# Modulation sums on four column strips of TensorE, and another order of the last expert pair's work

## The chip, the cores and the metric
The kernel runs on one core of a Trainium2 chip. The metric is device time in microseconds of one launch. The core's engines appear in the rows as PE (TensorE, the matrix engine) with PEld (its weight loads), DVE (VectorE), ACT (ScalarE), POOL (GpSimd) and SP (SyncE, which here only issues DMAs). Each engine takes its instructions in order, and they wait for each other by semaphores.

## The reference, cut to what matters
A trunk of two layers over 256 tokens of width 1024. Both layers get their shifts, scales and gates from one conditioning vector:

```python
cond = jax.nn.silu(c)
for i in range(DEPTH):                                  # 2 layers
    mod = (cond @ ada_w[i] + ada_b[i])[:, None, :]      # 1024 -> 6 * 1024
    sh1, sc1, g1, sh2, sc2, g2 = jnp.split(mod, 6, axis=-1)
    x = x + g1 * mixer(rms_norm(x, gain[i, 0]) * (1 + sc1) + sh1)      # layer 0 GLA, layer 1 FoX
    x = x + g2 * ffn(rms_norm(x, gain[i, 1]) * (1 + sc2) + sh2)        # layer 0 dense, layer 1 MoE
# MoE: y = sum over 8 experts of combine_e * ((silu(h Wg_e) * (h Wu_e)) Wd_e), two experts for each token
```

A dense or expert SwiGLU is 1024 to 3584 and back. All weights are float32.

## The kernel before, in words
Weights come in tiles `raw` of 1 MB (128 partitions x 2048 numbers) by one DMA each, issued on SP's queue at L203 in program order, through a ring of 7 buffers, 10 in the expert stage. For most products a tile is split into two rounded parts, `whi` (ACT, L224) and `wlo` (DVE, L226), and every product is three matmuls: high by high, high by low, low by high (L241 to L243 with the activations held in the array, L247 to L249 with the weights held). A planner orders the instructions of each engine: it simulates the program and picks, among what is ready, what comes first in the program; functions marked `urgent` go ahead of that.

The modulations. One modulation (i, j) is 1024 numbers. `ada_gen` makes ten of them during the GLA and dense stages, a step at a time between the weight tiles: DVE multiplies each row block of `ada_w` by the conditioning value of its partition and adds it up in `adacc` (128x1024, L320 and L322). What is left is a sum over the 128 partitions and a turn from a row into columns, since `mod` is kept as 128 partitions x 8. `end` does both: for nine of the ten, eight matmuls that hold a 128-column block of `adacc` in the array and move one column of ones (L309), and `ada_out` adds the bias (L261). A float32 matmul stands in the trace as two records, so eight matmuls are 16. The tenth modulation, g2, takes another way (L304). The call of `end` for a modulation comes two steps into the next one.

The experts. They go in four pairs, ranked by their number of tokens on the device. Of a pair, `Large` x has up to 128 tokens and goes by the split parts; `Small` y has up to 64 tokens, takes `raw` as it is in float32, and `mm_s` (L1256) computes the two halves of the output columns in two strips of 64 array columns. The 3584 columns go in four chunks c (1024, 1024, 1024, 512): `gu` computes gate and up, `finish` turns the product (`actT`) for the down product, and `down` adds chunk c to the expert's output `md`. For chunk 3, `gu` has four weight tiles for the two halves together (two gate, two up) and `down` has two. Behind the last `down` of an expert, `scatter_pre` and `scatter` (x), or `scatter_s` (y), scale the output, split it, send it back to the tokens by one-hot matmuls (`sc`) and add it to `xres` (L1232 for x, L1210 for y). What is to be done later lies in a list, `pend`; `flush` runs it. The order of a pair is x.gu(0), y.gu(0), then for c = 0 to 2: x.down(c), x.gu(c+1), y.down(c), y.gu(c+1); then x.down(3). y.down(3) comes after the next pair's first x.gu(0), or, in the last pair, right behind x.down(3). Then `store` writes the output.

Of the kernel before, what the change touches and what calls it, by code (L numbers as in the profile page):

```python
# [17 lines left out]
P = 128  # L18
T = 256
NB = 2  # L20
D = 1024
KD = 8
FF = 3584
NFC = 7
NCH = 4
E = 8
# [24 lines left out]
def trunk(ctx, tc, x, c, ada_w, ada_b, norm_gain, gla_w_in, gla_w_gate_up, gla_b_gate, gla_o_norm, gla_w_out,  # L51
          fox_w_in, fox_b_f, fox_q_norm, fox_k_norm, fox_w_out, ffn_w_gate, ffn_w_up, ffn_w_down,
          moe_w_router, moe_b_router, moe_w_gate, moe_w_up, moe_w_down, out):
    nc = tc.nc
# [31 lines left out]
    def wk_ps(name):  # L86
        return pwk["p"].tile([P, 512], F32, tag="wkp", name=name)
# [4 lines left out]
    def bcast(ap, n):  # L92
        return bass.AP(tensor=ap.tensor, offset=ap.offset, ap=[[0, P], [1, n]])
# [9 lines left out]
    ident = cst.tile([P, P], F32, name="ident")  # L103
    make_identity(nc, ident)
    ones = cst.tile([P, P], F32, name="ones")
# [13 lines left out]
    bias = adap.tile([P, 96], F32, name="bias")  # L119
# [74 lines left out]
    def unit(src, nk):  # L194

        p = rawp
        if more["p"]:
            p = rawp if more["n"] % NRING < 7 else more["p"]
            more["n"] += 1
        raw = p.tile([P, 2048], F32, tag="raw", name="raw")  # L200
        v = raw.rearrange("p (k f) -> p k f", k=nk)
        for s, dst in src:
            ld.dma_start(dst(v), s.rearrange("(k p) f -> p k f", p=P))  # L203
        return v
# [52 lines left out]
    def ada_out(i, j, ps):  # L257

        c = (6 * i + j) * KD
        m = mod[i, j] = cst.tile([P, KD], F32, name=f"mod_{i}_{j}")  # L260
        nc.vector.tensor_add(m, ps, bias[:, c:c + KD])  # L261
        if j in (1, 4):
            g = (2 * i + j // 3) * KD
            nc.vector.tensor_mul(m, m, gain[:, g:g + KD])
# [33 lines left out]
    def ada_gen(todo):  # L298
        def end(i, j, a):
            if (i, j) == (1, 5):  # L300
                ld.dma_start(g2, bcast(ada_b[1:2, 5 * D:6 * D], D))
                for h in range(2):
                    ps = wk_ps(f"g2_{h}")
                    nc.tensor.matmul(ps, ones, a[:, h * 512:(h + 1) * 512], start=True, stop=True)  # L304
                    nc.vector.tensor_add(g2[:, h * 512:(h + 1) * 512], g2[:, h * 512:(h + 1) * 512], ps)
                return
            ps = wk_ps(f"adat_{i}_{j}")
            for k in range(KD):
                nc.tensor.matmul(ps[:, k:k + 1], a[:, k * P:(k + 1) * P], ones[:, 0:1], start=True, stop=True)  # L309
            ada_out(i, j, ps[:, 0:KD])  # L310

        late = None
        for i, j in todo:
            a = ada["p"].tile([P, D], F32, tag="adacc", name=f"adacc_{i}_{j}", bufs=2)
            for u in range(4):
                raw = unit([(ada_w[i][u * 2 * P:(u + 1) * 2 * P, j * D:(j + 1) * D], lambda v: v)], 2)
                for kk in range(2):
                    k = 2 * u + kk
                    if k == 0:
                        nc.vector.tensor_scalar(a, raw[:, kk, :], csil[:, k:k + 1], None, op0=ALU.mult)  # L320
                    else:
                        nc.vector.scalar_tensor_tensor(a, raw[:, kk, :], csil[:, k:k + 1], a, op0=ALU.mult, op1=ALU.add)  # L322
                if u == 1 and late:
                    end(*late)
                    late = None
                yield
            late = (i, j, a)
        end(*late)


# [768 lines left out]
    def experts(norm, wr):  # L1099
        rest, hh, hl, pos, comb, cmi, weights, ranks, first, order, pos_s, comb_s, room = route(norm, wr)  # L1100
        a, s = norm.a(), norm.s()
# [86 lines left out]
        def flush():  # L1188
            todo, pend[:] = pend[:], []
            for f in todo:  # L1190
                f()
# [189 lines left out]
        for e in range(0, E, 2):  # L1381
            x = Large(e)
            x.gu(0)
            tail()
            if e == 0:
                gather(1, 1)
            y = Small(e + 1)
            y.gu(0)
            for c in range(NCH - 1):
                x.down(c)  # L1390
                x.gu(c + 1)
                if (e, c) == (0, 0):
                    weights()
                y.down(c)
                y.gu(c + 1)
            if e + 2 < E:
                gather(e + 2, e + 3)
            x.down(NCH - 1, flush if e + 2 == E else lambda: None)

            def tail(y=y):  # L1400
                y.down(NCH - 1, flush)
# [77 lines left out]
    with wk.phase("first"):  # L1479
# [30 lines left out]
        h, step = n0.apply("X")  # L1510
# [25 lines left out]
    with wk.phase("fox"):  # L1536
        n3 = Norm("moe", "X", lambda: mod[1, 4], lambda: mod[1, 3])
        wr = side_by_side(small["wr_raw"], E, "wr")
        with wk.phase("fox_groups"):
            go, last = fox(n2, small["wf_raw"], lambda: None)  # L1540
            out_proj(go, fox_w_out[0], lambda: mod[1, 2], "foxo", n3, last, 2, (1,))
        with tc.tile_pool(name="rawq", bufs=NRING - 7) as more["p"], wk.phase("experts"):
            xres, hh, hl, pos, comb, cmi, room = experts(n3, wr)
# [31 lines left out]
```

## Time and profile before
| | us |
|---|---|
| median of 3 runs (1474.64 to 1475.36) | 1474.78 |
| the profiled execution, its own time | 1478.52 |
| its span in the trace | 1476.8 |
| PE busy | 1419.3 |
| DVE busy | 961.7 |
| ACT busy | 695.1 |

The trace is one execution, taken by the hardware profiler. Times in rows are us from the start of the span. A timeline row gives start, length, engine, line, operation, out<-in, held*moved or shapes, the count merged into the row, and in brackets how long the engine stood idle before and what ended that. The clock is the one granted to TensorE as a share of 2.4 GHz, so 0.50 is 1.2 GHz.

### The profile page before, as it was taken

The numbers are of one execution on the slowest core, as the hardware profiler recorded it, in microseconds if no ns is written. First come the engines' busy times: TensorE is split into PE (matmuls) and PEld (weight loads), VectorE is DVE, ScalarE is ACT, GpSimd is POOL, SyncE is SP. The second block draws the span as 40 slices with busy tenths as digits, with TensorE's granted clock in tenths as the row PEclk, the third lists the DMA queues.
The fourth block names the chain that finished last, engine by engine and source line by source line (L and its number), as shares of the span: only waits on it lengthen the run. The fifth ranks groups of instructions, "written<-read, shape, count | busy, mean of one in ns | idle before, by whom it ended". The sixth has DMA issues, their size and how long they took to land.

```text
span 1476.8 us, 21633 instructions
## 1 busy us (share of the span) xinstructions
PE 1419.3 (96%) x8443; PEld 1073.4 (73%) x8443; DVE 961.7 (65%) x1292; ACT 695.1 (47%) x982; POOL 80.5 (5%) x87
## 2 busy tenths in 40 slices
PE   6999999999999998999999999999999999999996
PEld 2899999999999997864756664656475556475453
DVE  7786897778977786662744764556574456574353
ACT  3653644344565565552644463445264346254241
POOL 2000200000132124000000000000000000000000
PEclk9999999999999999899999999999999999999998
DMA  9996578898865432699999999999999999999994
GB/s 318 362 340 226 189 269 313 296 345 279 286 178 161 127 103 86 252 403 395 409 402 402 409 409 409 409 402 402 409 409 409 409 401 404 409 409 408 410 398 189
DMA packets 183000, 488.86 MB, mean 331 GB/s; under 512 B 10815, under 2 KB 51913, under 8 KB 182890
## 3 DMA queue, kind: packets, MB, share of 16 engines
q1 hardware_dynamic: 182602, 486.87, 87.7%
q8 instruction: 68, 1.11, 0.3%
q10 hardware_dynamic: 288, 0.52, 0.1%
q14 instruction: 42, 0.34, 0.1%
HBM read 486.32 MB, written 1.05 MB: 330 GB/s over the span
## 4 chain that ended last, share of the span: by engine, by line
PE 81%; DMA 9%; DVE 7%; issue 1%; SPq 1%; ACT 0%; DVEq 0%; ACTq 0%
PE mo L1256 8%; PE mo L243 6%; PE mo L241 6%; PE mo L242 6%; PE md L1256 6%; DMA raw<-in_moe_w_up_dram 4%; PE gu L247 3%; DVE wlo L226 3%; PE gu L249 3%; PE gu L248 3%; PE md L243 3%; DMA raw<-in_moe_w_down_dram 3%; PE md L242 3%; PE md L241 3%; PE dn L247 2%; PE dn L248 2%
## 5 line engine op out<-in xcount | busy, mean ns | idle before, releaser
L226 DVE TENSOR_TENSOR wlo<-raw,whi 128x1024 fp32r<-128x1024 f32 (+2 forms) x481 | 569.0, 1232 | 92.2 <-ACT whi L224 90.9
L224 ACT CAST whi<-raw 128x1024 fp32r<-128x1024 f32 (+2 forms) x491 | 487.5, 1051 | 262.4 <-PE gu L248 67.3
L1256 PE MATMUL mo<-raw,gs 128*64 128x512 f32 (+1 forms) x1024 | 203.7, 543 | 9.9 <-DMA raw<-in_moe_w_up_dram 8.4
L241 PE MATMUL mo<-whi,g 128*128 128x512 f32 x448 | 175.9, 393 | 0.0
L242 PE MATMUL mo<-whi,g 128*128 128x512 f32 x448 | 175.5, 392 | 0.0
L1256 PEld LDWEIGHTS mo<-raw,gs 128*64 128x64 f32 x1024 | 70.3, 137 | 131.1 <-issue 95.5
L243 PE MATMUL mo<-wlo,g 128*128 128x512 f32 x448 | 153.0, 399 | 1.0 <-DVE wlo L226 0.5
L1352 DVE TENSOR_TENSOR msg<-msg,mo 128x512 f32<-128x512 f32 (+1 forms) x16 | 9.9, 620 | 171.6 <-PE mo L1256 171.6
L243 PEld LDWEIGHTS mo<-wlo,g 128*128 128x128 f32 x448 | 83.2, 189 | 35.9 <-issue 13.8
L1256 PE MATMUL md<-raw,gs 128*64 128x512 f32 x448 | 108.8, 603 | 0.0
L241 PEld LDWEIGHTS mo<-whi,g 128*128 128x128 f32 x448 | 84.6, 189 | 19.2 <-issue 1.6
L242 PEld LDWEIGHTS mo<-whi,g 128*128 128x128 f32 x448 | 84.7, 189 | 18.1
L322 DVE SCALAR_TENSOR_TENSOR adacc<-raw,csil,adacc 128x1024 f32<-128x1024 f32 x70 | 90.0, 1286 | 10.3 <-DMA raw<-in_ada_w_dram 9.9
L249 PE MATMUL gu<-h_ffn_h,wlo 128*128 128x256 f32 x320 | 90.5, 284 | 0.0
L248 PE MATMUL gu<-h_ffn_l,whi 128*128 128x256 f32 x320 | 90.1, 282 | 0.0
L247 PE MATMUL gu<-h_ffn_h,whi 128*128 128x256 f32 x320 | 89.9, 283 | 0.0
L241 PE MATMUL md<-whi,act_h 128*128 128x512 f32 x192 | 76.7, 400 | 0.5 <-ACT whi L224 0.5
L242 PE MATMUL md<-whi,act_l 128*128 128x512 f32 x192 | 76.1, 397 | 0.0
L1350 ACT ACTIVATE msg<-mo 128x512 f32<-128x512 f32 (+1 forms) x16 | 8.7, 544 | 132.6 <-PE mo L1256 132.6
L1175 ACT CAST act_h<-actT 128x512 fp32r<-128x512 f32 x24 | 13.3, 589 | 116.2 <-PE actT L1240 116.2
L1256 PEld LDWEIGHTS md<-raw,gs 128*64 128x64 f32 x448 | 28.2, 136 | 51.5 <-issue 51.2
L243 PE MATMUL md<-wlo,act_h 128*128 128x512 f32 x192 | 62.2, 398 | 1.4 <-DVE wlo L226 1.3
(488 smaller groups left out, 2706.1 us busy)
## 6 DMA issues: line engine op xcount, KB each, us to landing
raw<-in_moe_w_gate_dram SPq DMA_DIRECT2D x112, 1024.0 KB, 17.1
raw<-in_moe_w_up_dram SPq DMA_DIRECT2D x112, 1024.0 KB, 16.3
raw<-in_moe_w_down_dram SPq DMA_DIRECT2D x112, 1024.0 KB, 16.9
raw<-in_ada_w_dram SPq DMA_DIRECT2D x48, 1024.0 KB, 7.1
raw<-in_fox_w_in_dram SPq DMA_DIRECT2D x16, 1024.0 KB, 5.9
raw<-in_ffn_w_gate_dram SPq DMA_DIRECT2D x14, 1024.0 KB, 5.3
raw<-in_ffn_w_up_dram SPq DMA_DIRECT2D x14, 1024.0 KB, 6.5
raw<-in_ffn_w_down_dram SPq DMA_DIRECT2D x14, 1024.0 KB, 5.3
```

What stands on the lines that cost most here:

```text
L224: nc.scalar.copy(hi[:, s], raw[:, s])
L226: (nc.gpsimd if i in pool else nc.vector).tensor_tensor(lo[:, s], raw[:, s], hi[:, s].bitcast(F32), op=ALU.subtract)
L241: nc.tensor.matmul(ps, ah, wh, start=first, stop=False)
L242: nc.tensor.matmul(ps, al, wh, start=False, stop=False)
L243: return nc.tensor.matmul(ps, ah, wl, start=False, stop=last)
L247: i = nc.tensor.matmul(ps, wh, ah, start=first, stop=False)
L248: nc.tensor.matmul(ps, wh, al, start=False, stop=False)
L249: nc.tensor.matmul(ps, wl, ah, start=False, stop=last)
L322: nc.vector.scalar_tensor_tensor(a, raw[:, kk, :], csil[:, k:k + 1], a, op0=ALU.mult, op1=ALU.add)
L1175: acts["i"] = nc.scalar.copy(ah, v)
L1256: nc.tensor.matmul(ps[64 * i:64 * (i + 1), 0:n], a, w[:, i * n:(i + 1) * n], start=first, stop=last)
L1352: nc.vector.tensor_mul(sg, sg, ps[:, 0:hw])
```

## The change
Two edits that do not touch each other. In `end`, the sum over partitions is four matmuls that hold 32 columns of ones and move 256 columns of `adacc`; the four write to four groups of 32 partitions of one PSUM tile, so that partition group q holds 32 copies of the numbers 256q to 256q + 255. ACT copies the 128x256 result into the first columns of `adacc`, two transposes turn it, and `ada_out` reads every 32nd column of their result. In the last pair alone, x.down(3) moves from behind y.gu(3) to between y.down(2) and y.gu(3), and the calls of `flush` move with it.

```diff
@@ ada_out
-        nc.vector.tensor_add(m, ps, bias[:, c:c + KD])
+        nc.vector.tensor_add(m.rearrange("p (q h) -> p q h", h=2), ps,
+                             bias[:, c:c + KD].rearrange("p (q h) -> p q h", h=2))
@@ ada_gen, end
-            ps = wk_ps(f"adat_{i}_{j}")
-            for k in range(KD):
-                nc.tensor.matmul(ps[:, k:k + 1], a[:, k * P:(k + 1) * P], ones[:, 0:1], start=True, stop=True)
-            ada_out(i, j, ps[:, 0:KD])
+
+            ps = wk_ps(f"adas_{i}_{j}")
+            for q in range(4):
+                nc.tensor.matmul(ps[32 * q:32 * (q + 1), 0:T], ones[:, 0:32], a[:, q * T:(q + 1) * T], start=True,
+                                 stop=True)
+            row = a[:, 0:T]
+            nc.scalar.copy(row, ps[:, 0:T])
+            pt = wk_ps(f"adat_{i}_{j}")
+            for h in range(2):
+                nc.tensor.transpose(pt[:, h * P:(h + 1) * P], row[:, h * P:(h + 1) * P], ident)
+            ada_out(i, j, pt[:, 0:T].rearrange("p (h q r) -> p q h r", h=2, q=4)[:, :, :, 0])
@@ experts, the loop over pairs
-                y.down(c)
+                end = e + 2 == E and c == NCH - 2
+                y.down(c, flush if end else lambda: None)
+                if end:
+                    x.down(NCH - 1)
                 y.gu(c + 1)
             if e + 2 < E:
                 gather(e + 2, e + 3)
-            x.down(NCH - 1, flush if e + 2 == E else lambda: None)
+                x.down(NCH - 1)
+            else:
+                flush()
```

## Rows read from the trace of the kernel before

**Rows 1.** The page's slices: 40 equal parts, busy tenths of the DMA engines.
```profile
DMA  9996578898865432699999999999999999999994
```

**Rows 2.** Windows of 37 us: PE, PEld, DVE, ACT, POOL busy, clock, DMA share, GB/s.
```profile
259.00:296.00 37.00, 37.00 (x314) 37.00 (x313) 26.70 (x26) 12.72 (x11) 0.00 (x0) 1.00 0.88 296
888.00:925.00 37.00, 36.14 (x166) 18.44 (x166) 15.02 (x17) 13.21 (x16) 0.00 (x0) 1.00 1.02 409
```

**Rows 3.** The tile adat: its matmuls in ns, and who waited for them.
```profile
L309 PE MATMUL adat<-ones,adacc x144: 164/250/352, 105.0 to 379.1; 128*128 128x1 f32 x144
...
  DVE mod L261: 7.2, 6
```

**Rows 4.** Timeline of the dense stage around one modulation's end.
```profile
286.27 0.28 PE L249 MATMUL gu<-h_ffn_h,wlo 128*128 128x256 f32 x1
286.39 1.84 PE L309 MATMUL adat<-ones,adacc 128*128 128x1 f32 x16
286.47 1.90 ACT L224 CAST whi<-raw 128x2048 fp32r<-128x2048 f32 x1 [4.51 <-PE gu L248]
...
288.10 0.37 PE L247 MATMUL gu<-h_ffn_h,whi 128*128 128x256 f32 x1
288.30 0.28 PE L248 MATMUL gu<-h_ffn_l,whi 128*128 128x256 f32 x1
```

**Rows 5.** Timeline behind the GLA stage, where two modulations end.
```profile
134.34 1.84 PE L309 MATMUL adat<-ones,adacc 128*128 128x1 f32 x16
...
136.68 3.04 PE L309 MATMUL adat<-ones,adacc 128*128 128x1 f32 x16
...
139.58 0.56 PE L247 MATMUL glao<-go_h,whi 128*128 128x256 f32 x1
...
143.78 0.35 PE L248 MATMUL glao<-go_l,whi 128*128 128x256 f32 x1
```

**Rows 6.** Windows of 1 us there, columns as in rows 2.
```profile
137.00:138.00 1.00, 1.00 (x7) 1.00 (x6) 0.17 (x1) 0.72 (x4) 0.00 (x0) 0.54 1.03 397
...
144.00:145.00 1.00, 1.00 (x10) 1.00 (x10) 0.00 (x0) 0.84 (x1) 0.00 (x0) 1.00 0.00 0
```

**Rows 7.** The tile adacc: g2's matmuls of 512 float32 columns, full width, in ns.
```profile
L304 PE MATMUL g<-adacc,ones x4: 590/592/592, 405.3 to 406.6; 128*128 128x512 f32 x4
```

**Rows 8.** Timeline of the last 41 us: PE, ACT and DVE.
```profile
1440.18 1.90 PE L1256 MATMUL mo<-raw,gs 128*64 128x256 f32 x16
...
1447.72 1.95 PE L1256 MATMUL mo<-raw,gs 128*64 128x256 f32 x16 [0.76 <-DMA raw<-in_moe_w_up_dram]
...
1450.27 0.44 PE L1362 MATMUL actT<-ident,msg 128*128 128x128 f32 x2 [0.59 <-DVE msg L1352]
1450.32 2.00 ACT L224 CAST whi<-raw 128x1024 fp32r<-128x1024 f32 x2 [5.63 <-DMA raw<-in_moe_w_down_dram]
...
1451.41 0.50 PE L241 MATMUL md<-whi,acs_h 128*128 128x512 f32 x1 [0.71 <-ACT whi L224]
...
1452.22 0.37 ACT L1363 COPY gs<-actT 128x256 f32<-128x256 f32 x1
...
1456.98 0.39 PE L243 MATMUL md<-wlo,acs_h 128*128 128x512 f32 x1
...
1457.30 1.94 PE L1256 MATMUL md<-raw,gs 128*64 128x512 f32 x8
...
1463.36 0.47 PE L1230 MATMUL sc<-yh,ohT 128*128 128x512 f32 x1 [0.70 <-DVE xres L1232]
...
1464.39 0.68 DVE L1198 TENSOR_TENSOR gs<-md,gs 128x512 f32<-128x512 f32 x1
...
1465.18 0.62 ACT L1199 CAST yh<-gs 128x512 fp32r<-128x512 f32 x1 [4.06 <-DVE gs L1198]
...
1466.31 0.68 DVE L1200 TENSOR_TENSOR yl<-gs,yh 128x512 fp32r<-128x512 f32 x1
```

**Rows 9.** Windows of 0.5 us where the last weights land, columns as in rows 2.
```profile
1457.00:1457.50 0.50, 0.50 (x4) 0.20 (x4) 0.10 (x1) 0.00 (x0) 0.00 (x0) 1.00 0.02 8
```

## The prediction
> **What bounds the kernel now.** I read the page's slices first, then windows by stage, then the timeline of the three places that the diff touches. The slices show two kernels in one: from the 18th slice to the 39th the DMA engines are busy throughout, before that they are not [rows 1]. The windows say what binds instead. In the dense stage PE is busy 37.00 us of 37 while DVE stands at 26.70, ACT at 12.72 and DMA at 0.88; in the expert stage DMA is at 1.02 and PE has some slack [rows 2]. So a microsecond taken from PE before the experts moves everything behind it forward, since the expert weights wait for the first expert to free the ring; a microsecond taken from PE inside the expert stage is worth nothing until the last weights have landed. The first edit lies in the first kind of stage, the second at the very end. I take 0.2%, 2.95 us, as what a measurement can tell from no change.
>
> **The modulation sums: what goes.** There are 144 records, nine runs of 16 [rows 3]. One run starts at 286.39 and the next product at 288.10, so it holds PE for 1.71 us, although each moves a single column. The product behind it comes 0.20 us before its successor where 0.12 is the pace, so the change of kind costs 0.08: 1.79 us a run [rows 4]. Eight runs at this price are 14.3 us (some are cut into pieces by other products, which costs no less). The ninth runs at half clock, from 136.68 to 139.58, 2.90 us [rows 5]. Together 17.2 us go.
>
> **What comes.** Four matmuls of 256 float32 columns, 8 records. The trace has no 32-column strip. Its nearest rows are the 256-column matmuls in 64-column strips, 16 records in 1.95 us or 0.122 each [rows 8], against 0.43 for 512 columns at full width (three steps from 405.3 to 406.6) [rows 7], hence 0.21 for 256. That two strips take 0.12 a record shows that the second record of one strip runs beside the first of the next. With the records in the order hi, lo, hi, lo, four strips in a row do the same, so I take 8 x 0.122 = 0.98. The bounds are 1.71 (8 x 0.213, no overlap) and 0.43 (all four strips at once, two rounds). Two transposes take 0.44 with their latency [rows 8]; a matmul that moves 128 columns behind others holds PE for about half of that, 0.22 the two. As there are now two visits to PE, the change of kind is paid twice, at 0.1: from 1456.98 to 1457.30, where a strip matmul follows one of full width, it is 0.32 us, and 0.25 on the way there (22 steps from 1451.41) [rows 8]. That makes 0.98 + 0.22 + 0.20 = 1.40 a run, 12.6 for nine, and 4.6 us saved. With the bounds in place of 0.98 it is -2.0 to +9.6.
>
> At this place the Trainium skill can be weighed against the rows. Its page TensorEngine Tiling (Array Packing), section Key Properties, says that tiles run independently and in parallel, and also that a change of the tiling mode drains the engine. By its first half a run's sums would take the 0.43 of the lower bound. By its second half each visit pays for a drain; the 0.07 us at 1457.30 agrees in sign, and no row shows more.
>
> The ACT copy is new in the chain: 128x256 took 0.37 us [rows 8]. ACT has room, but its casts last 1.90 and themselves wait for PE [rows 4]. If the planner puts other products between sums and transposes, this costs PE nothing. What it hides behind is thus the products of the stage. If that cover is missing, PE stands until ACT is through. Behind the transposes waits DVE's bias add, and behind that on DVE the `wlo` of the next weights; DVE already stood 7.2 us in six such waits [rows 3] while PE stayed full. I take 0.2 us of PE time a run, 1.8 in all; bounds 0 and one whole cast each, 17. The bias add with its other pattern still writes 128x8 once a run: nothing. The tile of sums and that of transposes need one PSUM buffer more for a moment, which I cost at nothing, as all this is before the experts' smaller pool.
>
> **The clock.** Behind the GLA stage two runs of one-column matmuls follow each other at 134.34 and 136.68 [rows 5], and the granted clock falls to 0.50 (1.2 GHz) at about 137; it is back at 1.00 in the window at 144 [rows 6]. From 139.58 to 143.78 there are 20 products [rows 5], 0.21 us each instead of 0.12: 1.8 us lost. Behind a single run elsewhere the products keep the usual pace [rows 4], and 64-column strips keep 1.00 for whole expert windows [rows 2]. As nearly no one-column matmul is left here, I expect no fall: 1.8 us saved; bounds 0 and 1.8 (the run's own half-clock price is already in the 17.2).
>
> **The last pair.** The same 1 MB tiles are loaded, only in another order; SP issues them in that order, and x's two `down` tiles pass y's four. The last bytes land at about 1457.1 either way [rows 9]. Before, both of x's tiles and both of y's are worked on behind the landing of x's first at 1450.3. DVE is then so busy with x's scatter that y's last step starts at 1464.39, and its `yl` starts at 1466.31 with no idle time before it, while `yh` ended at 1465.80 [rows 8]. After the change x is done earlier, and this wait of about 0.5 goes.
>
> What comes late next is PE. It is free at 1440.2, when the first gate tile has landed [rows 8]. I walk it from there. A tile lands every 2.6 us (1447.72 to 1450.32), so the place that x's first tile takes over is 1439.9. Its products start 1.1 us behind the landing, 23 of the 24 took 5.8 (1451.41 to 1457.2) and the last 0.2 more, so x.down(3) ends at 1447.0. y's four gate and up tiles cost 1.95 each, the `sc` matmuls of x about 1.4 for each half (four at 0.25, and changes of kind). Up's second tile, now at 1447.7, lands two tiles later, at 1452.9 [rows 8]. But PE, which has gate (to 1448.9), half a scatter and gate (1452.3), up (1454.2), half a scatter (1455.6), takes it up at 1455.6 only and ends at 1457.6. Product, transposes and ACT copy took from 1449.67 (1447.72 + 1.95) to the copy's possible end at 1451.1, some 1.4 with the last product's tail; so y.down(3) starts at 1459.0 and ends two tiles of 1.87 later at 1462.8. y's last step thus starts at 1462.8 rather than 1464.39, 1.6 earlier, and with the 0.5 from `yl` the edit saves 2.1 us. Bounds: were the landing to set the end, the last tile would be worked through by 1459.0 and 5.9 saved. If `sc` waits on DVE between PE's tiles as at 1463.36 (0.70 each, four of them, 2.8) [rows 8], 0.7 is lost.
>
> **Sum.** -4.6 + 1.8 - 1.8 - 2.1 = -6.7 us. The profiled execution took 1478.52, its span and 1.7 around it; so 1471.8, 0.45% less. Runs go by the median of 1474.78, 3.7 lower than that execution: 1474.78 - 6.7 = 1468.1 us.
>
> **The rivals.** *Four strips at once.* Each run's sums cost 0.43, not 0.98, and 9 x 0.55 = 5.0 more is saved: 1463.1. For it: two strips already overlap; against it: a strip's second record follows its first in the same columns. The Trainium skill, TensorEngine Tiling (Array Packing), Key Properties, states it as said above. 0.16.
>
> *The clock falls all the same*, since PE works in only 32 columns and in transposes there: 1469.9. 0.10.
>
> *The new order at the end brings nothing*, because PE meets the end as late as DVE did: 1470.2. PE had only some 3.5 us of waits for weights between 1440 and 1452, which speaks for it. 0.09.
>
> *The copy's wait takes the place of what is saved* (the other side). Place: the nine transposes behind ACT's casts. Without any wait the sum would be -8.5. A mean wait of 0.62 a run leaves a gain under 2.95, and one of 1.27 a run makes the kernel slower by more than 2.95; a whole cast each time (1.90) gives 1474.78 - 8.5 + 17.1 = 1483.4. For it: casts are long, and the planner's times are not the chip's. Against it: ACT is idle 24 us of 37 [rows 2], and PE has other ready products. Between the two bounds 0.14 (about 1474), beyond them 0.09 (about 1480).
>
> **How the numbers follow.** My forecast has the remaining 0.42, with its own range from 1465 to 1471. Faster by over 0.2%: 0.42 + 0.16 + 0.10 + 0.09 = 0.77; within it 0.14; slower 0.09. The range leaves out the worst waits and the last of the bounds on the fast side: 1461.5 to 1474.
>
> **What would show it.** The line of sums should have 72 records, those of one run within about 1 us; the transposes should start without PE standing before them; PE's windows from 137 to 144 should show a clock of 1.00; x's last `md` should end some 10 us before the last landing, and y's L1198 start 5.7 us behind that landing where it was 7.3 (1457.1 to 1464.39), the landing itself being moved only by what was saved before. The prediction is wrong if PE stands for ACT before most transposes, if the planner, given other instructions, orders the dense stage or the norms' edges worse by some microseconds, or if the last weights land later than the saved time says.

## The result, and the profile after

The kernel with both edits took 1466.72 us in the median of five runs, the kernel before 1475.36; the ratio is 0.9933, with a 95% interval from 0.9915 to 0.9951. Timed again beside other runs it was 0.9943 (0.9925 to 0.9960). That is 8 to 10 us where 6.7 was forecast, and inside the range. The profiled executions differ by more, 1476.8 against 1465.0 us of span, since that of before lay 3.2 us above its median.

First the sums. The timeline of PE and ACT around the first one, after the change:

```profile
103.25 0.59 PE L620 MATMUL o<-v,aT 128*128 128x256 f32 x2
...
103.78 0.64 PE L311 MATMUL adas<-adacc,ones 128*32 128x256 f32 x8
104.35 0.39 PE L241 MATMUL r<-whi,h_gla_h 128*128 128x256 f32 x1
104.49 0.37 ACT L314 COPY adacc<-adas 128x256 f32<-128x256 f32 x1 [0.40 <-PE adas L311]
104.57 0.28 PE L242 MATMUL r<-whi,h_gla_l 128*128 128x256 f32 x1
```

Eight records hold PE from 103.78 to 104.35, 0.57 us, where the one-column run held it for 1.71 [rows 4]. The windows of 0.05 us for this tile alone (columns as in rows 2, without DVE and POOL) tell why; the counts in brackets are the records in flight:

```profile
103.80:103.85 0.05, 0.05 (x4) 0.05 (x8) 0.00 (x0) 1.00 0.64 246
...
103.95:104.00 0.05, 0.05 (x4) 0.00 (x0) 0.00 (x0) 1.00 1.08 410
104.00:104.05 0.05, 0.05 (x8) 0.00 (x0) 0.00 (x0) 1.00 0.85 328
```

Four records run from the start; the other four join at 104.0, 0.2 us later, the time of 256 columns. The row does not name the strips, but the half sum below, of two strips, starts with two records and is joined by the other two after the same 0.2. So one record runs in each strip. A float32 matmul's two records are thus not worked off strip by strip: all first records go, then all second ones. Not every sum has this price. The timeline of PE in the dense stage:

```profile
246.72 0.28 PE L249 MATMUL gu<-h_ffn_h,wlo 128*128 128x256 f32 x1
246.93 0.62 PE L311 MATMUL adas<-adacc,ones 128*32 128x256 f32 x4
247.48 0.39 PE L247 MATMUL gu<-h_ffn_h,whi 128*128 128x256 f32 x1
247.71 0.28 PE L248 MATMUL gu<-h_ffn_l,whi 128*128 128x256 f32 x1
...
249.10 0.62 PE L311 MATMUL adas<-adacc,ones 128*32 128x256 f32 x4
249.65 0.38 PE L247 MATMUL gu<-h_ffn_h,whi 128*128 128x256 f32 x1
```

Here the planner put products between the second and the third strip. Half a sum takes 0.55 us, as long as a whole one. Three of the nine were cut like this. The windows of the first half, for the tile alone, columns as above:

```profile
247.10:247.15 0.05, 0.05 (x2) 0.00 (x0) 0.00 (x0) 1.00 0.00 0
247.15:247.20 0.05, 0.05 (x4) 0.00 (x0) 0.00 (x0) 1.00 0.00 0
```

The way into the strips has a price too. The product at 246.72 is followed after 0.21 us, and at 103.25 two records hold PE for 0.53 instead of 0.43; into the one-column run it was 0.12 [rows 4], nothing extra. With 0.09 in front and 0.10 behind (104.35 to 104.57 is 0.22), a sum in strips costs 0.76 us. The line of who waited, of the tile of sums, answers to the second of [rows 3]:

```profile
  ACT adacc L314: 1.0, 3
```

ACT waited for PE, and PE never for ACT's copy. Second the clock, by windows of 1 us (columns as in rows 2) that answer to [rows 6]:

```profile
137.00:138.00 1.00, 1.00 (x12) 0.76 (x14) 0.40 (x1) 1.00 (x4) 0.00 (x0) 1.00 0.26 100
138.00:139.00 1.00, 1.00 (x13) 0.66 (x6) 1.00 (x1) 0.67 (x3) 0.00 (x0) 1.00 0.08 31
...
190.00:191.00 1.00, 1.00 (x7) 1.00 (x6) 1.00 (x5) 0.00 (x0) 0.91 (x1) 0.50 1.19 406
```

There is no fall behind the GLA stage any more; one at 190 remains, where the kernel before had one at 196. Before also had one from 38 to 41 that this execution lacks; their windows at 39, before and after:

```profile
39.00:40.00 1.00, 1.00 (x5) 1.00 (x6) 1.00 (x3) 0.33 (x1) 0.00 (x0) 0.50 1.09 346
39.00:40.00 1.00, 1.00 (x10) 1.00 (x10) 1.00 (x3) 0.11 (x1) 0.00 (x0) 1.00 1.10 349
```

Third the end, first the timeline of PE, then that of DVE, then a window of 0.5 us:

```profile
1436.76 0.39 PE L243 MATMUL md<-wlo,acs_h 128*128 128x512 f32 x1
1437.08 1.95 PE L1264 MATMUL mo<-raw,gs 128*64 128x256 f32 x16
...
1445.88 1.95 PE L1264 MATMUL mo<-raw,gs 128*64 128x256 f32 x16
1448.42 0.44 PE L1370 MATMUL actT<-ident,msg 128*128 128x128 f32 x2 [0.59 <-DVE msg L1360]
1449.32 3.65 PE L1264 MATMUL md<-raw,gs 128*64 128x512 f32 x16 [0.46 <-ACT gs L1371]
```

```profile
1453.02 0.69 DVE L1206 TENSOR_TENSOR gs<-md,gs 128x512 f32<-128x512 f32 x1 [4.66 <-PE md L1264]
1454.45 0.69 DVE L1208 TENSOR_TENSOR yl<-gs,yh 128x512 fp32r<-128x512 f32 x1 [0.74 <-ACT yh L1207]
```

```profile
1447.50:1448.00 0.50, 0.33 (x4) 0.00 (x0) 0.06 (x1) 0.00 (x0) 0.00 (x0) 1.00 0.08 33
```

The last window with weights in flight ends at 1448.0 (1457.5 before [rows 9]). PE is busy almost without a pause from x's `down` through y's last up product, stands only in the chain of product, transposes and copy, and y's last step on DVE waits for PE, not the other way round. From the end of that window to the end of the span it is 17.0 us, before 19.3; I call this the tail. It is good to some 0.5 us.

### The profile page after: what moved, and what is told of

The parts are those of the page before. It is cut to its first block, busy times and chain, and to the rows that moved or that the text cites. A ratio compares the mean times of both kernels' runs of the same rounds, so it can differ in the third digit from the quotient of the medians.

```text
span 1465.0 us, 21546 instructions
## 1 busy us (share of the span) xinstructions
PE 1409.3 (96%) x8389; PEld 1056.6 (72%) x8389; DVE 963.2 (66%) x1292; ACT 697.6 (48%) x991; POOL 85.0 (6%) x87
## 4 chain that ended last, share of the span: by engine, by line
PE 80%; DMA 8%; DVE 8%; issue 1%; SPq 1%; ACT 1%; POOL 0%; DVEq 0%; ACTq 0%; POOLq 0%
PE mo L1264 9%; PE mo L243 6%; PE md L1264 6%; PE mo L241 6%; PE mo L242 6%; DVE wlo L226 4%; DMA raw<-in_moe_w_down_dram 3%; PE gu L247 3%; PE gu L249 3%; PE gu L248 3%; PE md L243 3%; PE md L242 3%; PE md L241 3%; DMA raw<-in_moe_w_up_dram 3%; PE dn L247 2%; PE dn L248 2%
```

## The experiments

The table gives for each kernel the ratio to the kernel before, and from its trace the end of the last window with weights in flight (landing), the tail, and the PE time of sums and transposes. The latter is, for each visit, the time from its first record to the start of the next product, plus what the step into the visit and the next product's own step have over their usual pace (0.12 us for most products). The expectations were worked out without the step into the strips: their 10.0, 8.0 and 7.4 us saved are 11.1, 8.7 and 6.3 here.

| kernel | ratio (95%) | landing | tail | PE for sums |
|---|---|---|---|---|
| before | 1 | 1457.5 | 19.3 | 17.4 |
| both edits | 0.9933 (0.9915 to 0.9951) | 1448.0 | 17.0 | 11.1 |
| both, again | 0.9943 (0.9925 to 0.9960) | 1450.5 | 16.8 | 11.1 |
| sums only | 0.9959 (0.9944 to 0.9973) | 1450.5 | 19.9 | 11.1 |
| order only | 0.9998 (0.9982 to 1.0014) | 1457.5 | 17.3 | as before |
| two sums only | 0.9967 (0.9954 to 0.9979) | 1450.0 | 19.3 | not summed |
| full width | 0.9988 (0.9976 to 1.0000) | 1455.5 | 16.9 | 17.4 |
| sums together | 0.9933 (0.9913 to 0.9953) | 1445.5 | 17.1 | 8.7 |
| and gap filled | 0.9922 (0.9905 to 0.9938) | 1448.0 | 16.2 | 8.7 |
| no last x scatter | one run | 1449.5 | 14.3 | not summed |

**The sums alone.** The order of the last pair is put back:

```diff
-                end = e + 2 == E and c == NCH - 2
-                y.down(c, flush if end else lambda: None)
-                if end:
-                    x.down(NCH - 1)
+                y.down(c)
...
-                x.down(NCH - 1)
-            else:
-                flush()
+            x.down(NCH - 1, flush if e + 2 == E else lambda: None)
```

> Only the modulation sums are changed; the last pair keeps its old order. Theory (the sums carry most, by PE time freed before the experts and by the clock that no longer falls behind the GLA stage; the two edits add up): 9.5 us off the profiled span of before at the last weights' landing, and the tail behind that landing 19.5 us long as before, so the run is some 7 to 9.5 us faster than before, and 2.3 us slower than both edits together. Rival (the planner's other order of the whole program made the gain, whichever edit set it off): less than 4 us faster, or as fast as both edits together.

The landing came 7.0 us earlier, less than the 9.5, and the tail stayed long. The windows of this execution (columns as in rows 2) show where the difference lies:

```profile
138.00:139.00 1.00, 1.00 (x12) 0.59 (x7) 1.00 (x1) 0.76 (x4) 0.00 (x0) 1.00 0.03 10
164.00:165.00 1.00, 1.00 (x6) 1.00 (x6) 1.00 (x3) 0.00 (x0) 0.85 (x1) 0.50 0.00 0
```

The clock held at 138, but stood at 0.50 from 162 to 169, twice as long as the later fall of the kernel with both edits. The sums carry most of the gain. The rival's "less than 4 us" is out: it is 6.0 by the ratio, 4.0 at the end of the interval. That the sums alone are as fast as both edits the run times do not exclude, since the intervals of 0.9959 and 0.9933 overlap; against it stands the tail, 19.9 as before and not 17.0.

**The order alone** is the other half, with the sums as before.

> Only the order of the last pair is changed; the sums are the old ones. Theory: nothing before the last pair moves (first gather at 591.6, last landing at 1457.4 in the trace, both within 0.5), the tail behind the landing shrinks from 19.5 to 17.2 us, and the run is 2.3 us faster than before. Rival (the order matters elsewhere, by the planner): the landing moves by more than 1 us, or the tail is as long as before.

The landing did not move and the tail fell to 17.3, so the trace bears the theory out. The run times do not resolve it: 0.9998 with an interval of 2.4 us to either side, which just takes in the 2 us of the tail. DVE's row, of y's last step, 5.3 us behind 1457.5:

```profile
1462.80 0.69 DVE L1198 TENSOR_TENSOR gs<-md,gs 128x512 f32<-128x512 f32 x1 [4.00 <-PE md L1256]
```

This execution has the old sums, and again the fall of the clock behind the GLA stage (window with columns as in rows 2):

```profile
138.00:139.00 1.00, 1.00 (x7) 1.00 (x6) 0.01 (x1) 0.00 (x0) 0.69 (x1) 0.50 0.27 100
```

**Two sums alone**, those that end behind the GLA stage; the order is the old one:

```diff
+            if (i, j) not in ((0, 4), (0, 3)):
+                ps = wk_ps(f"adat_{i}_{j}")
+                for k in range(KD):
+                    nc.tensor.matmul(ps[:, k:k + 1], a[:, k * P:(k + 1) * P], ones[:, 0:1], start=True, stop=True)
+                ada_out(i, j, ps[:, 0:KD].rearrange("p (q h) -> p q h", h=2))
+                return
```

> The old order of the last pair; of the nine modulation sums only the two that end behind the GLA stage, (0, 4) and (0, 3), go by the four strips, the other seven by one-column matmuls. Theory (the fall of the clock there came from the one-column matmuls): granted clock 1.00 from 130 to 150 us, the last product of that stage's output projection 4 to 5 us earlier than its 161.6 of before, and about that much of the run's time, half of what both edits bring. Rival (the fall has another cause, and only PE time counts): clock at 0.50 for some 6 us there as before, about 2 us saved.

The last product of that output projection started at 156.1 instead of 161.6, though 0.9 of these 5.5 us were there at its first product (128.6 against 129.5), and the window at 138 stands at 1.00:

```profile
138.00:139.00 1.00, 1.00 (x11) 0.93 (x8) 0.77 (x2) 1.00 (x1) 0.20 (x1) 1.00 0.00 0
```

The 0.9967 is half of the gain, as expected. Its landing is early beyond that: this execution also lacks the fall that before has near 196.

**Full width.** No strips; the modulations come out wrong, as the expectation says:

```diff
-                nc.tensor.matmul(ps[32 * q:32 * (q + 1), 0:T], ones[:, 0:32], a[:, q * T:(q + 1) * T], start=True,
-                                 stop=True)
+                nc.tensor.matmul(ps[:, 0:T], ones, a[:, q * T:(q + 1) * T], start=True, stop=True)
```

> Both edits, but each of a sum's four matmuls holds all 128 columns of ones and writes the same 128 partitions, so the later overwrite the earlier and the modulations are not the reference's; copy, transposes and the rest stay. Theory (a sum is cheap because the four strips run at once, in two rounds): 8 records of 0.213 take 1.7 us of PE a sum instead of 0.57, and the run is 9 x 1.1 = 10 us slower than with the strips, about as slow as before. Rival (what counts is that there are fewer and wider matmuls and no one-column ones, not the strips): within 2 us of the strips.

PE's timeline at the first sum:

```profile
103.84 0.59 PE L619 MATMUL o<-v,aT 128*128 128x256 f32 x2
104.27 1.89 PE L311 MATMUL adas<-adacc,ones 128*128 128x256 f32 x8
105.81 0.47 PE L241 MATMUL r<-whi,h_gla_h 128*128 128x256 f32 x1
106.12 0.28 PE L242 MATMUL r<-whi,h_gla_l 128*128 128x256 f32 x1
```

The step in is 0.43 for two records, so full width costs nothing there where the strips cost 0.09. The sum takes 1.54 us and has a dearer step behind it, 1.73 in all. Over the nine sums PE's time is 17.4, exactly that of the one-column form: the strips are the whole saving of PE time, and fewer, wider matmuls bring nothing by themselves. Against both edits the ratio is worse by 0.0045 to 0.0055, 6.6 to 8.1 us, near the 6.3 of PE time and under the 10 expected, since three cut sums and the steps in and out had cost the strips more than was reckoned. There is a second reading. The PE time is that of before, yet the clock does not fall at 138:

```profile
138.00:139.00 1.00, 1.00 (x9) 0.94 (x9) 0.00 (x0) 0.87 (x1) 0.00 (x0) 1.00 1.03 395
```

and the output projection's first and last products start 29.3 us apart (128.8 and 158.1) where it was 32.1 before (129.5 and 161.6). Of these 2.8 us, 1.0 is PE time of the two sums in between (3.9 against 4.9, as the second of before ran at half clock); the other 1.8 is what the slow clock had cost the products. The landing is 2.0 us earlier than before, too rough a figure to read this from, as other falls and waits go into it.

**Both edits, timed again.**

> Both edits as they are, timed again beside other runs of the kernel before, since single runs of one kernel here lie up to 10 us apart. Theory: ratio 0.993 to 0.995, that is 7.4 us less PE time and 1.8 us for the clock behind the GLA stage before the experts, and 2.2 us at the tail, less or more by where the clock falls in a run. Rival (the first comparison's 9.9 us was luck): ratio 0.996 or more, as the sums alone gave.

0.9943 is in the expected span. Its trace is that of the same program with a landing 2.5 us later. It has a fall of the clock from 38 to 41 that the first trace lacks, and 1.4 us of the 2.5 are there when the output projection starts (128.7 against 127.3). The rest, 1.2, arises up to the dense stage's `gu` (210.7 against 208.1). Both traces have a fall there, this one at 164 to 167:

```profile
165.00:166.00 1.00, 1.00 (x6) 1.00 (x6) 1.00 (x3) 0.11 (x1) 0.79 (x1) 0.50 0.00 0
```

But here PE also stands 3.5 us for DVE and POOL, in the first trace 2.5, and in that of before 2.4. With falls as many and as long as here at other places than 137, the trace of before is the better one to compare with: the landing is 7.0 us earlier, and the tail 2.5 shorter.

**The sums kept together.**

```diff
-            for q in range(4):
-                nc.tensor.matmul(...)
+            with tc.high_priority(3 * URGENT):
+                for q in range(4):
+                    nc.tensor.matmul(...)
```

> Both edits, and the four strip matmuls of a sum go ahead of all other work, so that none is placed between them. Theory (four records, two strips, cost 0.66 us and eight records, four strips, cost 0.67, and three of the nine sums were cut in two): all nine sums at 0.67, PE time of sums and transposes 8.0 to 8.3 us instead of 10.0, the last landing 2 us earlier than with both edits at a like clock. Rival (the order elsewhere takes it back, or the records overlap less than that): 9.5 us or more of PE time, or no earlier landing.

All nine sums now hold PE for 0.57 us without a cut:

```profile
290.08 0.28 PE L249 MATMUL gu<-h_ffn_h,wlo 128*128 128x256 f32 x1
290.29 0.64 PE L312 MATMUL adas<-adacc,ones 128*32 128x256 f32 x8
290.86 0.39 PE L247 MATMUL gu<-h_ffn_h,whi 128*128 128x256 f32 x1
```

With transposes and changes of kind they cost 8.7 us, 2.4 less than with both edits, and the landing is 2.5 us earlier than in the first trace of both edits, in which the clock falls as often and as long. The run times of the two do not differ by what they can tell.

**The gap filled.** On top of that, at the end of the last pair:

```diff
-                ps = wk_ps(f"sc_{e}_{hf}_{b}")
+                ps = (acc_ps if (e, hf) == (E - 2, 1) else wk_ps)(f"sc_{e}_{hf}_{b}")
...
-                            mm_s(ps, gs[:, k, :], w_u[:, kk, :], k == 0, k == KD - 1)
+                            first["up"] = mm_s(ps, gs[:, k, :], w_u[:, kk, :], k == 0, k == KD - 1)
...
-                flush()
+                with after(first["up"]):
+                    flush()
```

> As the kernel with the sums kept together, and at the end the second half of x's last scatter stands behind y's last up product instead of ahead of it, in two PSUM buffers of its own, so that its four matmuls fill PE's wait for product, transposes and copy. Theory (PE, not the last landing, sets the tail now): y's last step starts 1.0 us closer to the landing than the 5.1 us of both edits, tail 16.2 instead of 17.2 us. Rival (the landing sets it): tail unchanged; or the later transposes cost more than is gained: tail longer.

PE's timeline shows the four `sc` between y's up product and the transposes, with nothing idle:

```profile
1444.84 1.95 PE L1265 MATMUL mo<-raw,gs 128*64 128x256 f32 x16
1446.72 0.50 PE L1239 MATMUL sc<-yh,ohT 128*128 128x512 f32 x1
...
1447.76 0.38 PE L1372 MATMUL actT<-ident,msg 128*128 128x128 f32 x2
1448.60 3.65 PE L1265 MATMUL md<-raw,gs 128*64 128x512 f32 x16 [0.46 <-ACT gs L1373]
```

The tail is 16.2, as expected, 0.8 shorter; with 0.9922 this is the fastest of all versions by its median, 1465.42, though its interval overlaps those of both edits and of the sums together.

**Without x's last scatter.**

```diff
             def out(self, hf):
+                if self.e == E - 2:
+                    return
```

> Both edits, but the output of the last large expert is never scaled, sent back and added, so its share is missing from the result. Theory (behind the reordering it is PE's backlog, with x's eight scatter matmuls in it, that sets the end): y's last up product is finished 2.4 us earlier, then the landing of the last down tile binds, and the tail from landing to end shrinks from 17.2 to 14.8 us. Rival (the landing or the chain behind it sets the end already): within 0.5 us of 17.2.

The tail is 14.3, 2.7 shorter. PE now takes up y's last up tile behind a wait for its landing:

```profile
1444.81 1.95 PE L1264 MATMUL mo<-raw,gs 128*64 128x256 f32 x16 [0.33 <-DMA raw<-in_moe_w_up_dram]
```

So in the new order it is indeed PE, with x's scatter matmuls in it, that sets the end. This kernel also leaves out the scatter's work on DVE and ACT; but with both edits it is PE that DVE waits 4.66 us for before y's last step, and filling PE's gap alone had already shortened the tail. 2.7 us more lie between the tail of both edits and one in which PE keeps up with the landing.

## Why the prediction came out

*What goes* was sized at 17.2 us and measures 17.4.

*What comes* was sized at 12.6 and measures 11.1. The step that failed is "with the records in the order hi, lo, hi, lo, four strips in a row do the same": it carried the two strips' pace over to four. The records are ordered otherwise, four strips run at once, and a sum holds PE for 0.57 instead of 0.98. So the mechanism of the rival given 0.16 is what happened, at 0.57 where it named 0.43. By itself it would have saved 3.7 more. Three sums cut in two by the planner, at 0.75 for each further visit, gave 2.2 of that back, and a visit's changes of kind cost 0.19 where 0.1 was reckoned, 0.8 for nine sums. The transposes, 0.22 for two with their change of kind, were 0.1 cheaper than forecast, 0.9 for nine. The Trainium skill, TensorEngine Tiling (Array Packing), Key Properties, has tiles working in parallel, and the trace agrees (four records in flight at once). It also has a drain at a change of tiling mode, and the trace agrees: the step into the strips is 0.21 (246.72 to 246.93) where that into one-column matmuls of full width is 0.12 [rows 4].

*The copy's wait* was sized at 1.8 and measures nothing: PE has no wait for `adacc`. The rival on the other side did not come about, as the planner placed other products in between every time.

*The clock* was sized at 1.8. It does not fall behind the GLA stage in any of eight traces of seven kernels whose sums there are no longer one-column matmuls, and does in both traces (before, order alone) in which they are. Full width separates it from PE time, and gives the same 1.8. What I did not see is that other falls come and go from one execution to the next. They and PE's waits moved the landing of one program by 2.5 us (1448.0 and 1450.5), so one profile is a poor base for a sum.

*The last pair* was sized at 2.1, and the tails measure 2.3 (17.0 against 19.3), by the path that was walked: PE late next, the wait of `yl` gone. x's last `md` ends 8.5 us before the landing where some 10 were forecast, and y's last step starts 5.0 behind it where 5.7 were. The 3.5 us of waits for weights that spoke for "brings nothing" were misread: from 1440 to 1452 the trace of before has 1.75 for weights (0.23, 0.76 and 0.76) and 1.3 for DVE and ACT.

*The sum* by these terms is -6.3 - 1.8 - 2.3 = -10.4. The two profiled executions differ by 11.8; the fall at 38, which the one of before has and the one of after lacks, is the other 1.4. The second trace of both edits, with that fall, differs from before by 9.5, since PE's waits were 1.1 longer there. The run times give 8 to 10, with an interval from 7.2 to 12.5 for the first comparison.

How often the fall at 137 comes in executions of which no trace was kept is open, but probably not always. The three falls before the experts in the trace of before lower its mean clock by 0.005, to 0.986. Of the 33 executions of before that were timed beside the first experiments, ten have 0.989 or 0.990 and took 1473.1 to 1475.1 us; the twelve at 0.986 or less took 1478.4 to 1480.8. Where the fall does not come, the change cannot save its price (the 1.8, and the 1.4 by which the sum at half clock took longer than the others).

The forecast of 6.7 was near by luck rather than by its terms: the sums' term was 1.7 too small and the wait's 1.8 did not come, 3.5 us that would have been missed more clearly had the median moved as far as the traces.

## What to carry to other kernels

A sum over partitions that stands in a stage bound by TensorE was cheapest, of the three forms tried here, as four 32-column strips of ones (0.76 us and 0.22 for the transposes, against 1.73 and 0.22 at full width, and 1.79 by one-column matmuls, which need none), if the four matmuls are kept next to each other: half of them cost as much as all. Where the last work of a program follows the last load, put first what has the longest chain behind it, and then look again for what is late next: here the order exchanged DVE's backlog for PE's and gained 2.3 us of a possible 5. A gain read off two profiles needs the timed runs beside it.

## What was not expected of the hardware

A float32 matmul of 256 columns in a 32-column strip leaves the other strips free for its whole length: two records of each of four strips took 0.57 us, two records of each of two strips 0.55. With 128 columns held the same eight took 1.54. Going into the strips cost 0.09, into full-width float32 nothing. And the granted clock falls to 0.50 at different places in executions of one program: with both edits at 189 to 193 in one, at 38 to 41 and 164 to 167 in the other, with spans of 1465.0 and 1467.3. Before the fall at 164 PE had run twelve one-column matmuls of the norm, from 162.79 on; before that at 189 it had stood 2.50 us for DVE. Neither brings a fall every time: the first trace has the same twelve from 160.38 on, and the full-width kernel a stand of 2.52 until 192.11, with the clock at 1.00 behind them.
